# New duration formulas in the planner that orders projections, attention and output projection of a hybrid decoder block

## The chip, the core and the metric

The kernel runs on one core of a Trainium2 chip. The metric is the device time of one execution in microseconds (us). Five engines work from queues of their own, each in the order in which the program issues to it: TensorE (PE, matrix products and transposes), VectorE (DVE), ScalarE (ACT), GpSimd (POOL) and SyncE (SP, which here only issues transfers). An instruction that waits holds up all that stand behind it in its queue.

## What is computed

One block on 1024 tokens of width 1024, float32 (cut to what matters):

```python
h = rmsnorm(x, g_mix_norm)
sb_q, sb_k, sb_v, fx_q, fx_k, fx_v, f_logit, m_q, gate_logit = split(h @ w_in)
o_sb  = stick_breaking_attention(sb_q, sb_k, sb_v)              # 8 heads of 64, causal
o_fox = forgetting_attention(rms(fx_q), rms(fx_k), fx_v, F)     # 8 heads of 64, causal
o_mem = memory_attention(rms(m_q), mk, mv)                      # 4 heads of 128, 256 tokens
gates = sigmoid(gate_logit)                                     # 3 x 1024 columns
merged = gates[0]*(o_sb @ w_sb) + gates[1]*(o_fox @ w_fox) + gates[2]*(o_mem @ w_mem)
x = x + merged @ w_out
u = relu(rmsnorm(x, g_mlp_norm) @ w_ff_up)                      # 1024 -> 4096
x = x + (u*u) @ w_ff_down
```

## The kernel before, in words

Every float32 operand of a product is split into a high part in a shorter format (made by ACT) and a low remainder (made by DVE: operand minus high part), and each product is done three times: high by high, high by low, low by high. So a weight tile `raw`, `ra` or `rb` becomes a pair: `ha`/`la`, `hb`/`lb` or `hc`/`lc`. PE has banks of 128x512 numbers for results: `pp` (three), `sc` (two), `tr` (two), `pv` (one). The large products (the unit products of L1466, the output projection of L2234, the MLP) use a scheme of Strassen's kind: sums and differences of quarters go into seven products, called P1 to P7 in the output projection.

The order of nearly all instructions up to the MLP's first products isn't written out. It comes from a planner in the program (class `Machine`, L186 on), which runs when the kernel is built. Each step of the algorithm is a process that asks for an operation on an engine (`Op`, with an estimated cost), for a buffer (`Get`), or for an event. The planner simulates time: an engine that comes free takes the operation that is ready and due first (due is the time at which it was asked for plus a constant `late` of its process), is busy for its cost, and hands its result on after a fixed tail. An operation of ACT that needs another function table is put off for up to 4.0 us as long as others of the present table are ready (`KEEP`). The order in which the simulation starts operations is the order in which the instructions are issued to the engines; at run time the chip keeps that order, and waits only where data or a buffer isn't ready. Costs change no instruction, only the order (and, since ACT's order changes, the points at which its function table is loaded).

There are two such plans. The first covers the prologue (norm of x, transposes at L475, warm-up transposes at L425), the projections (L1154 for values, gates and branches; L1466 for unit products), the attention (scores and weights at L834 to L944, softmax sums at L622 and L624, memory attention at L657) and two branches. It ends with the fetches of the last branch's operand: heads' outputs `r` are read back (L1673), a second part is fetched (`low_scr`, L1676) and added (L1678), the reciprocal sums are fetched (`l_scr`, L1682) and multiplied in (L1685), and the product is split (L1064 and L1065). The second plan covers the last branch, the output projection, the residual adds (`residual`), the second norm (`normed`: the squares at L2259, the sum at L2278, the root at L373 to L387, the scaling at L2291 on ACT and L2293 on DVE), the turning of the normed rows (`turn_half`, L2316: four transposes of 128x128 into one bank) and the first products of the MLP (L1992). The rest of the MLP, from about 1085 us on, stands in a written order.

All of the costs that the change touches come from three functions of the number of columns, in us: `mm_time` for a product on PE, `act_time` for ACT and `dve_time` for DVE. The cost of transfers (`transfer`, L296: 250 bytes per ns in one pipe, and 2.0 us) stays as it is.

Of the kernel before, what the change touches and what calls it, by code (L numbers as in the profile page):

```python
# [43 lines left out]
def tile_hybrid_block(  # L44
# [240 lines left out]
    spawn = machine.spawn  # L285

    def mm_time(*cols):
        return sum(0.004 + 0.000445 * m for m in cols)

    def act_time(*cols):  # L290
        return sum(0.08 + 0.00083 * m for m in cols)

    def dve_time(*cols):
        return sum(0.08 + 0.00105 * m for m in cols)

    def transfer(fn, size, issue=0.1, rate=250e3, queue_="SP"):  # L296

# [50 lines left out]

    SMALL = 0.19
    PIECE = mm_time(512) * 3  # L350

    def banks(tag):
# [77 lines left out]
    def norm(keys, late, after=None):  # L430
# [21 lines left out]
        for i, key in enumerate(keys):  # L452
            xt, ri, s = x_in[key][0], r[:, i:i + 1], key[1]
            yield spread_
            evs = []
            for k4 in range(2):
                cs = slice(k4 * 512, k4 * 512 + 512) if first else slice(0, D)
                if first or k4 == 0:
                    last = yield Op("DVE", dve_time(512 if first else D), lambda: nc.vector.scalar_tensor_tensor(
                        xt[:, cs], xt[:, cs], ri, gb[:, cs], ALU.mult, ALU.mult), goes_on=True)  # L460
                evs.append(spawn(norm_half(key, xt, k4, last), late))
            for ev in evs:
                yield ev
            XT.put(xt)
            machine.fire((h_made if key[0] == "x" else m_made)[s])

    def norm_half(key, xt, k4, scaled):

        yield scaled
        s, cs = key[1], slice(k4 * 512, k4 * 512 + 512)  # L470
        tr = yield Get(TR)

        def turn():
            for j in range(4):
                nc.tensor.transpose(tr[:, j * P:(j + 1) * P], xt[:, cs][:, j * P:(j + 1) * P], ident)  # L475
        yield Op("PE", 0.44, turn)
        tr4 = tr.rearrange("p (k s) -> p k s", s=P)
        ks4 = slice(4 * k4, 4 * k4 + 4)
        if key[0] == "x":
            hi, lo = (t[:, ks4, s * P:(s + 1) * P] for t in (hTh, hTl))  # L480
        else:
            hi, lo = (t[:, ks4, :] for t in mem_T[s])
        yield Op("ACT", act_time(512), lambda: nc.scalar.activation(hi, tr4, AF.Copy))
        yield Op("DVE", dve_time(512), lambda: nc.vector.tensor_tensor(lo, tr4, f32(hi), ALU.subtract))
        TR.put(tr)
        if key[0] == "x":
            machine.fire(half_made[s, k4])
# [46 lines left out]
    def sums_T():  # L534
        for k in range(4):
            (b11, b12), (b21, b22) = (tuple(tuple(t[:, 4 * k2 + k, c * 512:(c + 1) * 512] for t in (hTh, hTl))
                                            for c in range(2)) for k2 in range(2))
            t1, t2, w_ = yield Get(SN, 3)

            def first():  # L540
                nc.vector.tensor_tensor(t1, f32(b12[0]), f32(b11[0]), ALU.subtract)
                nc.vector.tensor_tensor(w_, f32(b12[1]), f32(b11[1]), ALU.subtract)
                nc.vector.tensor_tensor(t1, t1, w_, ALU.add)

            def second():
                nc.vector.tensor_tensor(t2, f32(b22[0]), t1, ALU.subtract)
                nc.vector.tensor_tensor(t2, t2, f32(b22[1]), ALU.add)

            def third():
                nc.vector.tensor_tensor(w_, t2, f32(b11[0]), ALU.subtract)  # L550
                nc.vector.tensor_tensor(w_, w_, f32(b11[1]), ALU.subtract)
            yield Op("DVE", dve_time(512, 512, 512), first)
            yield Op("DVE", dve_time(512, 512), second)
            two = [spawn(both("P6", k, t2)), spawn(both("P5", k, t1), 2.0)]
            yield Op("DVE", dve_time(512, 512), third)
            two.append(spawn(both("P7", k, w_), 1.0))
            for ev in two:
                yield ev
            SN.put(t1, t2, w_)
# [59 lines left out]
    def sums_kept(h0):  # L619

        cols = fn[:, 8 * h0:8 * h0 + 16]
        yield Op("DVE", SMALL, lambda: nc.vector.reciprocal(cols, cols))  # L622
        tr = yield Get(TR)
        yield Op("PE", 0.12, lambda: nc.tensor.transpose(tr[:16, :P], cols, ident))  # L624
        t = yield Get(OB)
        yield Op("ACT", act_time(P), lambda: nc.scalar.activation(t[:16, :P], tr[:16, :P], AF.Copy))
        TR.put(tr)
        yield Op("SP", 0.1, lambda: nc.sync.dma_start(
            l_scr[h0:h0 + 2, :].rearrange("h (i p) -> (h i) p", p=P), t[:16, :P]), 2.5)
        OB.put(t)  # L630

    def mem_attention(h, half, kv, q):
# [8 lines left out]
        def scores_of(t2):  # L641
            sc = yield Get(SC)
            mx = st[:, 4 + 2 * t2:6 + 2 * t2]

            def scores():
                for j in range(2):
                    ts_ = slice((2 * t2 + j) * P, (2 * t2 + j + 1) * P)
                    mm3(sc[:, j * MEM:(j + 1) * MEM],
                        [((qh[:, ts_], ql[:, ts_]), (kh[:, h2, :], kl[:, h2, :]))])

            def maxima():
                nc.vector.tensor_reduce(mx, sc.rearrange("p (t m) -> p t m", m=MEM), AX.X, ALU.max, negate=True)

            def exps():
                for j in range(2):
                    t = 2 * t2 + j
                    nc.scalar.activation(pr[:, t, :], sc[:, j * MEM:(j + 1) * MEM], AF.Exp,  # L657
                                         bias=mx[:, j:j + 1], accum_out=l[:, t:t + 1])
            yield Op("PE", 6 * mm_time(256), scores)
            yield Op("DVE", dve_time(512), maxima)  # L660
            yield Op("ACT", act_time(256, 256) + 0.34, exps, table=AF.Exp)
            SC.put(sc)
# [15 lines left out]
        def block(j):  # L678
            if j == 0:
                pv[0] = yield Get(PV)  # L680
            else:
                yield turned[0]
            tr = yield Get(TR)

            def turn():
                for t in range(4):
                    nc.tensor.transpose(tr[:, t * P:(t + 1) * P], pr[:, t, j * P:(j + 1) * P], ident)
            yield Op("PE", 0.44, turn)
            machine.fire(turned[j])
            ph = yield Get(PH)  # L690
            yield Op("ACT", act_time(512), lambda: nc.scalar.activation(ph, tr, AF.Copy))
            pl = yield Get(PL)
            yield Op("DVE", dve_time(512), lambda: nc.vector.tensor_tensor(pl, tr, f32(ph), ALU.subtract))
            TR.put(tr)
            yield products_[j]
            cs = slice(h2 * P, (h2 + 1) * P)
            ab = passes((vh[:, j, cs], vl[:, j, cs]), (ph, pl))
            result = yield Op("PE", 3 * mm_time(512), products(pv[0], ab, j == 0, j == 1), goes_on=True)
            machine.fire(products_[j + 1])
            yield result  # L700
            PH.put(ph)
            PL.put(pl)
# [2032 lines left out]
```

## Time and profile before

| | |
|---|---|
| time, median of 3 runs | 1667.45 us (1667.15 to 1668.06) |
| profiled execution, its own time | 1668.89 us |
| span of that execution in the profile | 1667.1 us |
| PE busy, products and transposes | 1654.5 us, 9118 instructions |
| DVE busy | 1292.5 us, 2079 instructions |
| ACT busy | 848.9 us, 1474 instructions |
| POOL busy | 256.3 us, 440 instructions |
| transfers | 284.32 MB, mean 171 GB/s |

The profile gives, for each engine, when each instruction ran and what ended the idle time before it. Durations of products overlap: a product of 512 columns is listed with 389 ns, though the next may begin sooner. A stretch of the time can be asked for by itself; its row gives the busy time and count of each engine, the clock granted to PE as a share of full speed, the share in which transfers ran, and the bytes that they moved.

### The profile page before, as it was taken

To read this page: it belongs to the slowest core of one execution; us is meant where nothing else is said; L and a number is where in the kernel's file an instruction comes from. 1 tells how busy PE (TensorE), PEld (TensorE's weight loads), DVE (VectorE), ACT (ScalarE), POOL (GpSimd) and SP (SyncE) were. 2 spreads that over 40 slices of the span, in tenths; PEclk is the share of its full clock that TensorE was granted. 3 is DMA by queue.
4 is the path that set the end of the run, shared out by engine and by line. 5 is a ranking of instruction groups with operands and counts; after the bars stand their busy time and mean duration, and the time that the engine had idled before them with its cause. 6 is when DMAs were issued, how large, how long until landed. Compare 5 with 4: busy or idle time off the path is not lost.

```text
span 1667.1 us, 24994 instructions
## 1 busy us (share of the span) xinstructions
PE 1654.5 (99%) x9118; PEld 1434.6 (86%) x9118; DVE 1292.5 (78%) x2079; ACT 848.9 (51%) x1474; POOL 256.3 (15%) x440
## 2 busy tenths in 40 slices
PE   9999999999999999999999999999999999999999
PEld 9998899998888888888888887878888888888887
DVE  7978778855459889868878798987777776787875
ACT  6445555535458898877761446533333345333331
POOL 0001000000153142245400011011122120000000
PEclk9999999999999999999999999999999999999999
DMA  7445534468474455577747643144444475564532
GB/s 247 149 161 170 165 114 137 141 182 255 140 237 145 147 160 162 140 222 222 244 142 215 219 168 104 58 158 150 148 158 158 151 275 211 181 213 169 202 126 76
DMA packets 142222, 284.32 MB, mean 171 GB/s; under 512 B 16914, under 2 KB 53330, under 8 KB 142099
## 3 DMA queue, kind: packets, MB, share of 16 engines
q1 hardware_dynamic: 110562, 183.08, 32.5%
q0 software_dynamic: 31536, 99.64, 19.9%
q8 instruction: 72, 1.18, 0.3%
q14 instruction: 52, 0.42, 0.1%
HBM read 189.83 MB, written 92.83 MB: 170 GB/s over the span
## 4 chain that ended last, share of the span: by engine, by line
PE 72%; issue 14%; DVE 7%; POOL 3%; DMA 3%; ACT 1%; SPq 0%; POOLq 0%; ACTq 0%; DVEq 0%
PE pp L1466 11%; PE pp L1154 10%; PE sc L1466 7%; PE pp L2672 7%; PE sc L1154 6%; PE tr L927 4%; PE tr L2672 4%; PE sc L2672 4%; POOL s_scr L2009 3%; PE pv L1466 3%; PE pv L2672 2%; PE sc L944 2%; PE pp L944 2%; DVE h L1928 2%; DVE tmp L1928 1%
## 5 line engine op out<-in xcount | busy, mean ns | idle before, releaser
L1992 PE MATMUL pp<-h,oh 128*128 128x512 f32 x384 | 118.7, 390 | 1.2 <-ACT cu L2077 0.9
L934 DVE TENSOR_TENSOR ptl<-tr,pth 128x512 fp32r<-128x512 f32 (+1 forms) x160 | 99.0, 628 | 23.9 <-ACT pth L932 23.1
L932 ACT ACTIVATE pth<-tr 128x512 fp32r<-128x512 f32 (+1 forms) x160 | 87.4, 557 | 33.5 <-PE sc L944 14.6
L1992 PEld LDWEIGHTS pp<-h,oh 128*128 128x128 f32 x384 | 71.9, 188 | 17.2 <-ACT cu L2077 1.7
L1383 POOL DMA_DIRECT2D raw<-w_in x32 | 24.2, 757 | 394.8 <-DVE la L1065 207.6
L1992 PE MATMUL pp<-h,ol 128*128 128x512 f32 x192 | 74.9, 390 | 0.0
L853 DVE TENSOR_TENSOR_SCAN e<-r,e 128x384 f32<-128x384 f32 (+3 forms) x64 | 66.3, 1044 | 6.8 <-ACT e L838 6.4
L2672 PE MATMUL pp<-h,h 128*128 128x512 f32 x288 | 66.6, 389 | 0.0
L2672 PE MATMUL pp<-sop,sop 128*128 128x512 f32 x288 | 66.6, 389 | 0.0
L2672 PEld LDWEIGHTS pp<-sop,sop 128*128 128x128 f32 x288 | 54.1, 188 | 11.2
L2672 PEld LDWEIGHTS pp<-h,h 128*128 128x128 f32 x288 | 54.1, 188 | 11.2
L927 PE MATMUL tr<-ident,e 128*128 128x128 f32 x416 | 62.5, 272 | 0.0
L927 PEld LDWEIGHTS tr<-ident,e 128*128 128x128 f32 x416 | 50.5, 140 | 9.9 <-DVE ptl L934 0.2
L2009 POOL DMA_DIRECT2D s_scr<-cu x48 | 26.1, 544 | 191.7 <-DVE cu L1999 183.6
L1014 POOL DMA_DIRECT2D h<-sbk_scr x64 | 33.3, 526 | 95.5 <-PE pv L151 29.5
L944 PE MATMUL sc<-pth,v 128*128 128x256 f32 (+1 forms) x170 | 47.4, 301 | 0.0
L2587 ACT ACTIVATE h<-t 128x2048 fp32r<-128x2048 f32 (+1 forms) x9 | 15.4, 1725 | 60.2 <-DVE t L1928 56.1
L1154 PE MATMUL sc<-h,hc 128*128 128x512 f32 (+1 forms) x154 | 44.8, 375 | 0.0
L1928 DVE TENSOR_TENSOR x<-x,pp 128x512 f32<-128x512 f32 x39 | 26.6, 682 | 22.8 <-PE pp L2672 22.8
L1065 DVE TENSOR_TENSOR lb<-raw,hb 128x1024 fp32r<-128x1024 f32 x20 | 24.5, 1223 | 25.6 <-ACT hb L1064 25.5
L2009 POOL DMA_DIRECT2D s_scr<-s x60 | 32.5, 542 | 71.4 <-DVE s L1928 64.8
L1992 PEld LDWEIGHTS pp<-h,ol 128*128 128x128 f32 x192 | 36.0, 188 | 8.1 <-DVE ol L1928 0.6
(792 smaller groups left out, 5540.3 us busy)
## 6 DMA issues: line engine op xcount, KB each, us to landing
ur<-s_scr SPq DMA_DIRECT2D x26, 1024.0 KB
raw<-w_in POOLq DMA_DIRECT2D x32, 512.0 KB, 4.8
raw<-w_up SPq DMA_DIRECT2D x60, 256.0 KB
s_scr<-s POOLq DMA_DIRECT2D x60, 256.0 KB, 2.7
g<-w_down SPq DMA_DIRECT2D x14, 1024.0 KB
s_scr<-cu POOLq DMA_DIRECT2D x48, 256.0 KB, 2.9
h<-sbk_scr POOLq DMA_DIRECT2D x64, 128.0 KB, 3.1
o<-gate_scr SPq DMA_DIRECT2D x32, 256.0 KB
```

Source lines behind the costliest of these rows:

```text
L853: nc.vector.tensor_tensor_scan(out=back, data0=rho[:, :u][:, ::-1], data1=back, initial=0.0 if last else beta[:, c + u:c + u + 1], op0=ALU ...
L927: nc.tensor.transpose(tr[:, jj * 256 + a * P:jj * 256 + (a + 1) * P], es[a][:, j * P:(j + 1) * P], ident)
L932: yield Op("ACT", act_time(512 - lo_c), lambda: nc.scalar.activation(ph[:, lo_c:], tr[:, lo_c:], AF.Copy))
L934: yield Op("DVE", dve_time(512 - lo_c), lambda: nc.vector.tensor_tensor(pl[:, lo_c:], tr[:, lo_c:], f32(ph[:, lo_c:]), ALU.subtract))
L944: nc.tensor.matmul(pv[0][:, c_:256], pair.v[:, j, b, :], p_[:, jj * 256 + c_:(jj + 1) * 256], start=(k == 0 and n_ == 0 and i == 0), stop= ...
L1014: nc.gpsimd.dma_start(f32(t[k][rows_, :]), src)
L1154: nc.tensor.matmul(ps, a_, b_, start=(first and i == 0), stop=(last and i == n - 1))
L1466: nc.tensor.matmul(out_, a_, b_, start=(first and n == 0 and j == 0), stop=(last and n == 3 and j == len(todo) - 1), skip_group_check=True)
L1928: nc.vector.tensor_tensor(out_, a_, b_, op)
L1992: nc.tensor.matmul(ps, w[a_][:, k * P:(k + 1) * P], h[b_][k], start=(first and k == 0 and i == 0), stop=(last and k == 3 and i == 2), skip ...
L2009: nc.gpsimd.dma_start(s_scr[r0:r0 + P, :], t)
L2672: nc.tensor.matmul(ps, a_[:, c, qs], b_[:, c, :], start=(kind in ("P1", "P2", "P7") and c == 0 and i == 0), stop=(kind in ("P2", "P4", "P3 ...
```

## The change

The constants of the three formulas are replaced. Nothing else is edited.

```diff
     def mm_time(*cols):
-        return sum(0.004 + 0.000445 * m for m in cols)
+        return sum(0.0133 + 0.0004167 * m for m in cols)
 
     def act_time(*cols):
-        return sum(0.08 + 0.00083 * m for m in cols)
+        return sum(0.09 + 0.00093 * m for m in cols)
 
     def dve_time(*cols):
-        return sum(0.08 + 0.00105 * m for m in cols)
+        return sum(0.07 + 0.00113 * m for m in cols)
```

By these, a product of 512 columns is planned with 0.227 us where it was 0.232, one of 256 with 0.120 (0.118); an operation of 512 columns on ACT with 0.566 (0.505) and on DVE with 0.649 (0.618); one of 1024 columns with 1.042 (0.930) and 1.227 (1.155). So PE is planned a little quicker on wide products, and ACT and DVE slower. The instructions stay the same ones on PE, DVE, POOL and SP. ACT has two more table loads, 26 instead of 24: one more at L657 (exponentials of the memory attention) and one more at L837 (the first step of the stick-breaking weights). The order moves on all engines, in many places by a few rows. Three places follow.

**PE, where the second norm's first rows are turned.** `L2316` are the transposes; `L2234` with `sc_9651` and `sc_9652` are products of the output projection that follow the `pv_9655` ones. Before:

```order
L2234 MATMUL pv_9655<-ha_9904,ol_9896 128x512
L2234 MATMUL sc_9651<-hb_10013,cu_9931 128x512
L2234 MATMUL sc_9651<-lb_10015,cu_9931 128x512
L2234 MATMUL sc_9651<-hb_10013,cu_9935 128x512
L2316 MATMUL pp_9648<-ident,h_9632 128x128 x4
L2316 MATMUL pp_9649<-ident,h_9632 128x128 x4
L2234 MATMUL sc_9651<-hb_10013,cu_9932 128x512
L2234 MATMUL sc_9651<-lb_10015,cu_9932 128x512
L2234 MATMUL sc_9651<-hb_10013,cu_9936 128x512
L2316 MATMUL pp_9650<-ident,h_9632 128x128 x4
```

And now, from the seventh product after `pv_9655` on:

```order
L2234 MATMUL sc_9651<-ra_9998,cu_9963 128x512
L2234 MATMUL sc_9651<-rb_10000,cu_9963 128x512
L2234 MATMUL sc_9651<-ra_9998,cu_9967 128x512
L2234 MATMUL sc_9651<-ra_9998,cu_9964 128x512
L2234 MATMUL sc_9651<-rb_10000,cu_9964 128x512
L2234 MATMUL sc_9651<-ra_9998,cu_9968 128x512
L2234 MATMUL sc_9652<-hb_9997,cu_9961 128x512
L2234 MATMUL sc_9652<-lb_9999,cu_9961 128x512
L2234 MATMUL sc_9652<-hb_9997,cu_9965 128x512
L2316 MATMUL pp_9648<-ident,h_9632 128x128 x4
L2316 MATMUL pp_9649<-ident,h_9632 128x128 x4
L2234 MATMUL sc_9652<-hb_9997,cu_9962 128x512
```

Between the last `pv_9655` product and the first turn there stood three products; now there stand fifteen (the six not shown are the first six of `sc_9651`).

**DVE, on the way to the first turn's operand.** `h_9632` and `h_9633` are rows of the residual, `L2278` to `L387` the sum and root of the norm, `L2293` the scaling; `h_9959` and `h_9936` are sums of quarters of an MLP weight, `ol` low parts for P4. Before:

```order
L1928 TENSOR_TENSOR h_9632<-h_9632,pp_9649 128x512
L1928 TENSOR_TENSOR h_9959<-h_9958 128x512
L1928 TENSOR_TENSOR h_9959<-h_9958,h_9959 128x512
L2278 TENSOR_REDUCE st_10079<-fn 128x2
L1928 TENSOR_TENSOR h_9633<-h_9633,pp_9650 128x512
L378 TENSOR_SCALAR st_10091<-st_10079 128x2
L381 RECIPROCAL st_10084<-st_10084 128x2
L385 TENSOR_TENSOR st_10092<-st_10084 128x2
L386 TENSOR_TENSOR st_10092<-st_10092,st_10091 128x2
L387 SCALAR_TENSOR_TENSOR st_10093<-st_10092,st_10084 128x2
L2293 SCALAR_TENSOR_TENSOR h_9632<-h_9632,st_10093,gb_9636 128x512 x2
```

And now:

```order
L1928 TENSOR_TENSOR ol_10028<-g_7040,oh_10024 128x512
L1928 TENSOR_TENSOR h_9633<-h_9633,pp_9650 128x512
L1928 TENSOR_TENSOR ol_10029<-g_7041,oh_10025 128x512
L378 TENSOR_SCALAR st_10081<-st_10073 128x2
L1928 TENSOR_TENSOR ol_10030<-g_7041,oh_10026 128x512
L381 RECIPROCAL st_10076<-st_10076 128x2
L385 TENSOR_TENSOR st_10082<-st_10076 128x2
L386 TENSOR_TENSOR st_10082<-st_10082,st_10081 128x2
L387 SCALAR_TENSOR_TENSOR st_10083<-st_10082,st_10076 128x2
L1928 TENSOR_TENSOR h_9633<-h_9633,pv_9655 128x512
L1928 TENSOR_TENSOR h_9936<-h_9935,h_9936 128x512
L2293 SCALAR_TENSOR_TENSOR h_9632<-h_9632,st_10083,gb_9636 128x512
```

The four low parts for P4, which stood ahead of this place, now stand in the chain; the sums and products that stood ahead of the residual add moved out of it, and two operations of 512 columns come between L387 and L2293.

**ACT, at the first weights of the second pair's values.** `hc_169<-rb_166` is the high part of these weights, for which PE's products at L1154 wait; `L1064 h_...<-sn` are high parts of another operand, `L1647` empties a gate's bank. Before:

```order
L1064 ACTIVATE h_757<-sn_150 128x512
L1064 ACTIVATE h_755<-sn_149 128x512
L1647 ACTIVATE sn_142<-sc_137 128x512
L1064 ACTIVATE hc_169<-rb_166 128x1056
L1064 ACTIVATE h_759<-sn_141 128x512
```

And now:

```order
L1647 ACTIVATE sn_142<-sc_137 128x512
L1064 ACTIVATE hc_169<-rb_166 128x1056
L1064 ACTIVATE h_747<-sn_150 128x512
L1064 ACTIVATE h_745<-sn_149 128x512
L1064 ACTIVATE ha_163<-ra_164 128x1056
```

The two high parts from `sn`, which stood ahead of the bank's emptying and of the weights, now stand behind both.

## Prediction

> **What bounds the kernel now.** I read the page first.
>
> ```profile
> span 1667.1 us, 24994 instructions
> PE 1654.5 (99%) x9118; PEld 1434.6 (86%) x9118; DVE 1292.5 (78%) x2079; ACT 848.9 (51%) x1474; POOL 256.3 (15%) x440
> ```
>
> PE works 1654.5 of 1667.1 us. The change leaves PE's instructions as they are, so the work doesn't shrink; a new order can only win what PE loses to waits (12.6 us) and to a lower clock, or add to it. So I asked where PE is idle: a table by stretches of the program, where the column after the window is PE's busy time.
>
> ```profile
> 0.00:25.00 25.00, 23.00 (x168) 21.96 (x169) 17.10 (x44) 16.42 (x31) 0.70 (x6) 1.00 0.96 333
> 55.00:60.00 5.00, 4.30 (x33) 3.89 (x32) 4.98 (x8) 2.96 (x5) 0.00 (x0) 1.00 0.95 288
> 475.00:880.00 405.00, 404.21 (x2528) 356.38 (x2527) 331.59 (x710) 317.26 (x710) 137.95 (x250) 1.00 0.61 181
> 880.00:1012.00 132.00, 131.44 (x580) 108.48 (x579) 115.14 (x162) 50.32 (x72) 10.56 (x7) 1.00 0.57 192
> 1012.00:1028.00 16.00, 13.05 (x60) 10.71 (x58) 14.86 (x31) 10.35 (x22) 0.00 (x0) 0.89 0.47 148
> 1085.00:1110.00 25.00, 23.77 (x101) 18.39 (x100) 21.75 (x33) 8.58 (x16) 4.88 (x9) 1.00 0.44 147
> ```
>
> Idle by difference: 2.00 at the start, 0.70 at 55 to 60, 0.79 in the whole attention (475 to 880), 0.56 in branches and first half of the output projection, 2.95 at 1012 to 1028, 1.23 at 1085 to 1110. Most of the rest lies after 1110, in the written order, which the change doesn't touch. The waits of PE say for whom:
>
> ```profile
> PE pp L2316 <- ACT h L2291: 3.0, 1, 3.0
> PE pp L1992 <- ACT cu L2077: 0.9, 2, 0.7
> PE pv L879 <- DVE st L884: 0.7, 1, 0.7
> PE pp L1154 <- DVE lc L1065: 0.6, 1, 0.6
> PE sc L2234 <- DVE rb L1928: 0.6, 1, 0.6
> ```
>
> One wait is worth more than the others together: the first turn of normed rows. Its stretch in steps, with the clock as the number after POOL's:
>
> ```profile
> 1017.00:1020.10 3.10, 0.55 (x3) 0.13 (x1) 2.96 (x11) 2.11 (x6) 0.00 (x0) 1.00 0.70 202
> 1020.10:1021.30 1.20, 0.79 (x6) 0.80 (x7) 1.20 (x3) 1.20 (x2) 0.00 (x0) 0.84 1.10 203
> 1021.30:1022.50 1.20, 1.20 (x6) 1.10 (x6) 1.20 (x2) 1.20 (x4) 0.00 (x0) 0.50 0.90 328
> 1022.50:1023.70 1.20, 1.20 (x6) 0.90 (x5) 0.95 (x3) 1.20 (x3) 0.00 (x0) 0.50 1.04 401
> 1023.70:1025.00 1.30, 1.30 (x7) 1.17 (x6) 1.05 (x2) 1.30 (x4) 0.00 (x0) 0.76 0.23 82
> ```
>
> After the wait PE counts as busy, but at a granted clock of 0.50 to 0.84. Lost to that: 1.20 x 0.16 + 1.20 x 0.50 + 1.20 x 0.50 + 1.30 x 0.24 = 1.70 us. So **this place costs 2.95 + 1.70 = 4.65 us**.
>
> **The turn, step by step.** The timeline there (start, duration, engine, line):
>
> ```profile
> 1017.16 0.39 PE L2234 MATMUL sc<-hb,cu 128*128 128x512 f32 x1
> 1018.94 0.60 ACT L2259 ACTIVATE pp<-h 128x512 f32<-128x512 f32 x1 [0.30 <-DVE h L1928]
> 1019.47 0.16 DVE L387 SCALAR_TENSOR_TENSOR st<-st,st 128x2 f32<-128x2 f32 x1
> 1019.67 1.41 DVE L2293 SCALAR_TENSOR_TENSOR h<-h,st,gb 128x512 f32<-128x512 f32 x2
> 1019.73 0.72 ACT L2291 ACTIVATE h<-h,st 128x512 f32<-128x512 f32 x1
> 1020.36 1.04 ACT L2136 ACTIVATE hc<-h 128x1024 fp32r<-128x1024 f32 x1
> 1020.51 1.20 PE L2316 MATMUL pp<-ident,h 128*128 128x128 f32 x6 [2.95 <-ACT h L2291]
> ```
>
> PE has issued its third product by 1017.39 and then stands until 1020.51, for ACT's scaling, which follows DVE's L387 (end 1019.63). The new order puts twelve more products ahead of the turn. What one of 512 columns costs PE comes from a stretch in which all are such:
>
> ```profile
> 1120.00:1142.70 22.70, 22.70 (x102) 18.81 (x101) 18.07 (x28) 7.03 (x13) 4.34 (x8) 1.00 0.48 162
> ```
>
> 22.70 / 100 (102 are counted with those cut at both ends) is 0.227 us, so PE now comes to the turn at 1017.39 + 12 x 0.227 = 1020.11. The operands: on DVE the same work stands ahead of L387 as before but for one sum of 512 columns, about 0.68 less by the rows of such operations (L2293: 1.41 for two), so L387 ends near 1019.0 to 1019.1. On ACT the high part L2136 (1.04) now stands ahead of the first L2291. L2259 follows its residual add, which ends some 1.2 earlier, near 1017.7, since one low part and the root's steps now lie behind that add; L2259 (0.60 and its read of 0.19) ends near 1018.5, L2136 near 1019.5, the first L2291 (0.72) at 1020.0 to 1020.3. The first turn waits 0 to 0.2. The second needs DVE's L2293, behind two operations of 512 columns: 1019.05 + 3 x 0.65 = 1021.0, against PE at 1020.6: 0.4 more. Together 0.4 to 0.7, and I take 0.65. Two shorter waits don't look like one of 2.95; the wait of 0.6 for rb (row above) is the nearest in size, and there the granted clock stayed up:
>
> ```profile
> 973.50:978.00 4.50, 3.94 (x18) 2.93 (x17) 4.50 (x7) 0.88 (x2) 0.00 (x0) 1.00 0.05 19
> ```
>
> So the turn goes from 4.65 to 0.65: **-4.0**. Until the end of the output projection everything on PE is then 4.0 earlier, and what is late next is DVE. It has room for that in the 57 us after the turn (51.19 of 57), with the end of the projection inside them:
>
> ```profile
> 1028.00:1085.00 57.00, 57.00 (x278) 47.33 (x276) 51.19 (x90) 33.40 (x61) 7.43 (x8) 1.00 0.17 61
> ```
>
> 5.8 us idle against 4.0: enough, and then the waits of 1085 to 1110 stay as they are. If that cover were gone, up to 4.0 would come back there.
>
> The Trainium skill ("TensorE: Matmul & The Clock Gate", Part 1: The HAM clock gate) says the array falls to half clock after an idle window of about 3.4 us and needs about 3.4 us of work to rise, in windows that run freely. The trace agrees in part: 2.95 us of idling sufficed, and the 0.50 lasted about 3 us. By that page short waits would cost nothing but themselves, as the row at 973 has it; the sum is the same.
>
> **The first weights of the second pair's values.**
>
> ```profile
> 53.31 1.15 ACT L1064 ACTIVATE h<-sn 128x512 fp32r<-128x512 f32 x2 [4.24 <-DVE sn L547]
> 54.85 1.07 ACT L1064 ACTIVATE hc<-rb 128x1056 fp32r<-128x1056 f32 x1
> 55.95 1.26 DVE L1065 TENSOR_TENSOR lc<-rb,hc 128x1056 fp32r<-128x1056 f32 x1
> 57.27 0.39 PE L1154 MATMUL pp<-lc,h 128*128 128x264 f32 x1 [0.64 <-DVE lc L1065]
> ```
>
> ACT idles 4.24 us for `sn`, does two high parts, empties a bank, then makes `hc`; `lc` ends at 57.21, and PE waits. In the new order bank and `hc` stand ahead of the two high parts. ACT can then start them inside the 4.24, so `lc` no longer ends last: **-0.7** by the idle of 55 to 60, and up to -1.1 with the small delays of the products behind it. I take -0.9. What is late next is those high parts, by ACT's 0.58 and 1.07; their users stand well behind on PE.
>
> **Start (0 to 25).** DVE's and PE's first steps change places: the first product's low part comes later, the transposes earlier. Followed row by row the first rows of products end within 0.2 of where they did. I take 0, between -0.4 and +0.4.
>
> **Attention.** Here the order moves most: counted in PE work from the start (each product of the order at its own duration, 0.227 for 512 columns), the last score product goes from 693 to 709 and the last product with values (L944) from 863 to 876, so that ACT and DVE have some 13 to 16 us more for the same work. That can win no more than the 0.79 that PE idles there. Against it stand the two more table loads on ACT:
>
> ```profile
> L657 ACT ACT_TABLE_LOAD x8 | 10.3, 1283 | 0.1
> L837 ACT ACT_TABLE_LOAD x7 | 9.0, 1283 | 0.1
> ```
>
> 2 x 1.28 = 2.57 us of ACT. ACT works 317 of the 405 us of that stretch, so 88 us of gaps hide them; without that cover they would cost 2.57. The range is -0.8 (all waits gone) to +2.6, and nearest is 0, since PE lost only one wait in 2528 products in an order that knew less of the durations.
>
> The Trainium skill ("ScalarE: Activation LUTs", What ACT_TABLE_LOAD costs) counts a drain of 1.38 us beside the 1.28, so 5.3 us for two, which speaks against this change. The trace has only the 1.28, with 0.1 idle ahead of it. By the page the upper end would be +5.3 and the value still 0, inside the same 88 us.
>
> **From attention to the last branch.** The work that PE can do without the last pair's operand shrinks: behind L624, 111 products (25.2 us) stand ahead of the last branch's first use where 171 (38.8 us) stood. The last pair's way, as now seen:
>
> ```profile
> 894.63 1.09 SPq L1682 DMA_DIRECT2D e<-l_scr  x2
> ...
> 901.73 1.23 DVE L1685 TENSOR_TENSOR r<-r,e 128x1024 f32<-128x1024 f32 x1 [0.63 <-DMA e<-l_scr]
> ```
>
> 7.1 us from issue to use, and now 15 us to spare. In the new order, from L624 on: on DVE the sum L1678 runs behind an eviction and `lb` at +14.2 to +15.3; SP issues the two fetches of `l_scr` at +15.5 behind three gate fetches; landing +22.6; L1685 to +23.8; splits at +26.7 and +27.9 behind two more evictions. PE uses them at +27.5 and +30.2. **0.85 us to spare**, so 0, and each us beyond that costs one. A slow fetch is seen in the chain:
>
> ```profile
> 729.43 8.29 DMA r<-o_scr
> ```
>
> At 8.29 instead of 7.1 PE would wait 0.3. I take +0.2, between 0 and +1.5.
>
> **Sum.** -4.0 - 0.9 + 0 + 0 + 0.2 = -4.7 on the profiled execution's 1668.89 us: 1664.2. That execution was 1.44 above the median of 1667.45, so the median comes to **1662.8 us**. The measurement can tell about 0.2%, 3.3 us, from no change.
>
> **Rivals**, in medians. (a) *The turn's gain is given back on DVE.* DVE is busy 14.86 of 16 us at the turn; if the projection's end comes 4.0 earlier but the splits behind it don't, the waits at 1085 to 1110 grow by up to 4.0: 1666.8, the same. For: only 5.8 us are free there. Against: these lie ahead of the written part. 0.14. (b) *The turn waits longer and the clock falls all the same.* If ACT's L2136 or the two operations ahead of L2293 run later than I count, by 1 us, and the clock's 1.70 is lost again: 1662.8 + 2.7 = 1665.5, the same. For: ACT has 1.04 more in the chain. Against: the row at 973. 0.12. (c) *The last pair's operand decides.* It is on a chain of two fetches, three DVE steps and two evictions. If `l_scr` takes twice its 7.1 us, since three gate fetches and the output projection's weights now go with it, and L1685 misses its place behind one pair of evictions (1.4), PE waits 8.5 - 0.85 = 7.65, and the clock falls for 1.70: 1662.8 - 0.2 + 9.35 = 1672.0, **slower**; it decides from some 7 us of lateness on. For: cover of 15 us is gone. Against: of the fetch now only 0.63 is waited for, and only by DVE. 0.10. (d) *Nothing but scattered waits changes places*: both gains are real in the order, but new waits of the size of the 0.6 to 0.9 rows turn up in 9118 rearranged products, five of them: 1662.8 + 3.5 = 1666.3, the same. 0.06.
>
> **How the numbers follow.** My forecast has 0.58, with 1660.9 to 1664.5 as its own range (the ends of the terms: start 0.4, attention 0.8, weights 0.2, turn 0.5 downward; the junction's 1.3 and 0.4 upward). The range must leave out no more than 2 in 10: 1660.5 to 1668.5 takes in (a), (b) and (d). Faster means under 1664.1: 0.60. Within 0.2%: 0.29. Slower than 1670.8: 0.11, (c) and a little for what I don't see.
>
> **What would show it.** Turn right: PE's wait for L2291 under 0.4, one for L2293 under 0.6, clock 1.00 throughout. Weights right: no wait of L1154 for `lc`. Junction right: no wait of L1154 in the 30 us behind the last L624. (a) shows as waits of L1992 above 1.3 us in all; (c) as a wait of L1154 for L1065 with `r` before the last branch. What would make it wrong most simply is a wait of several us at a place where PE lost nothing before.

## The result, and the profile after

The changed kernel takes **1683.57 us** (median of 5 runs, 1682.91 to 1684.17), the kernel before 1667.54 us in the same series: a ratio of 1.0093, with a 95% interval of 1.0078 to 1.0108. It is 16 us slower; 4.7 us faster was forecast, and the range ended at 1668.5. The two executions that were profiled lie 14.1 us apart (1682.98 and 1668.89 us). The page of the profile of the changed kernel:

```profile
span 1681.2 us, 24988 instructions
PE 1657.2 (99%) x9118; PEld 1432.0 (85%) x9118; DVE 1297.0 (77%) x2079; ACT 853.7 (51%) x1476; POOL 254.8 (15%) x440
```

PE's work is the same to 0.2%, and the span is 14.1 us longer: PE waits more. The same stretches as before the change, in the same columns (PE's busy time stands after the window). The first turn of normed rows now starts at 1035.7 us, 15.2 later than before, so its stretch is 1027 to 1043 here, where it was 1012 to 1028:

```profile
0.00:25.00 25.00, 21.43 (x171) 20.93 (x172) 15.88 (x38) 15.60 (x29) 0.70 (x6) 1.00 0.94 336
25.00:55.00 30.00, 28.28 (x235) 27.47 (x235) 23.36 (x50) 16.74 (x34) 0.00 (x0) 1.00 0.47 139
55.00:60.00 5.00, 5.00 (x44) 5.00 (x43) 4.96 (x7) 3.33 (x6) 0.00 (x0) 1.00 0.73 234
475.00:880.00 405.00, 396.28 (x2439) 346.26 (x2439) 322.35 (x688) 310.16 (x686) 138.26 (x251) 1.00 0.59 178
1027.00:1043.00 16.00, 15.61 (x75) 12.52 (x74) 15.79 (x31) 10.02 (x22) 1.30 (x1) 1.00 0.45 149
```

The two places on which the forecast was built behave as it said: at 55 to 60 PE is never idle (0.70 before), and at the turn it is idle for 0.39 us (2.95) at a clock of 1.00 (0.89). But the attention, 475 to 880, which had 0.79 us of idle PE, has 8.72, and 25 to 55, which had none, has 1.72. (0 to 25 has 3.57 for 2.00, but loses no more than before when it is counted from start to start, as in the table below: 4.3 against 4.5.) PE's waits name the places:

```profile
PE tr L927 <- DVE ptl L934: 6.2, 7, 1.7
PE tr L475 <- DVE xt L459: 1.7, 1, 1.7
PE pp L149 <- ACT es L838: 1.4, 1, 1.4
PE pp L944 <- DVE ptl L934: 1.2, 2, 0.7
PE tr L475 <- DVE g L484: 1.1, 1, 1.1
PE pp L2316 <- ACT tmp L2323: 0.6, 1, 0.6
PE pp L2316 <- DVE h L2293: 0.4, 1, 0.4
```

The first, third and fourth row are the attention's own steps (transposing the weights, multiplying them with the values). None of these was in the list before. Stretch by stretch, first of the kernel before, then of the changed one:

```profile
710.00:730.00 20.00, 20.00 (x130) 17.68 (x128) 12.02 (x33) 15.49 (x35) 10.93 (x21) 1.00 0.69 192
730.00:750.00 20.00, 19.31 (x112) 16.20 (x111) 15.45 (x42) 14.38 (x33) 9.15 (x17) 1.00 0.87 268
```

```profile
710.00:730.00 20.00, 14.85 (x91) 11.75 (x90) 17.11 (x38) 17.62 (x39) 14.22 (x27) 1.00 0.68 203
730.00:750.00 20.00, 16.44 (x111) 13.47 (x110) 15.02 (x41) 16.66 (x37) 10.53 (x20) 1.00 0.83 229
```

8.7 of the 40 us are idle. What is missing there shows when one asks for the products of L1154 alone. In this part of the program most of those are projections of gates and branches: they depend on nothing of the attention that is still running, and the planner gives them to PE only when no other step is ready for it (they are marked `side`). I call them spare products. (The same line also has the memory attention's own products with its weights `pth` and `ptl`, which aren't spare.) Before, then after (PE's busy time with that line alone):

```profile
690.00:710.00 20.00, 11.76 (x45) 7.73 (x43) 1.00 0.65 183
710.00:730.00 20.00, 11.54 (x43) 7.45 (x43) 1.00 0.69 192
730.00:750.00 20.00, 10.05 (x37) 6.16 (x35) 1.00 0.87 268
```

```profile
690.00:710.00 20.00, 12.21 (x48) 8.72 (x48) 1.00 0.22 71
710.00:730.00 20.00, 2.15 (x8) 0.99 (x6) 1.00 0.68 203
730.00:750.00 20.00, 2.84 (x10) 1.62 (x11) 1.00 0.83 229
```

From 710 to 750 PE had 80 products of this line and now has 18, and 12 of the 18 are the memory attention's own (6 of the 80). Of the spare ones, the last for a gate (`g`) and the first for the memory branch (`ha`) stand so in the changed kernel (durations in ns, then the first and the last start):

```profile
L1154 PE MATMUL pv<-g,lb x4: 389/393/395, 706.7 to 710.0; 128*128 128x512 f32 x4
L1154 PE MATMUL sc<-ha,hc x1: 395/395/395, 743.8 to 743.8; 128*128 128x512 f32 x1
```

From 710.0 to 743.8 no spare product starts, some 34 us; before, the two were at 738.1 and 738.3. The spare products aren't gone; they have run already. Counted in the order, 182 us of products of L1154 stood ahead of the 780th attention product, and 202 us stand there now. The next ones belong to the memory branch, which opens only when the memory attention's outputs are back. In between PE has nothing but the attention, and goes at the pace of its chain through ACT and DVE. A piece of that chain of waits:

```profile
711.00 1.28 ACT L837
712.58 0.37 ACT e L838
712.95 0.49 ACT r L837
713.44 0.49 ACT e L838
713.93 0.49 ACT pth L691
```

The first line is a table load; then sigmoids and copies stand on the path one after another, with PE idle.

For all runs below, what PE loses is counted from the start of one product to the start of the next, against 0.227 us for 512 columns, 0.177 for 384, 0.123 for 264, 0.120 for 256 and 0.109 for a transpose; so it holds idle time and slow products alike. In us, by stretch of each run's own profile (between 60 and 475, and from 1135 on, the sums are under 1 in these kernels except for the first of them in `issue_intervals`, 2.0; the stretches don't move with the program, so in runs that come there some 14 us late a wait can fall into the next column):

| run | 0–60 | 475–690 | 690–790 | 790–950 | 950–1010 | 1010–1060 | 1060–1135 | all |
|---|---|---|---|---|---|---|---|---|
| before | 5.7 | 1.1 | 1.9 | 0.8 | 0.8 | 5.1 | 2.4 | 17.3 |
| after | 6.8 | 1.0 | 13.7 | 2.7 | 0.9 | 2.7 | 4.2 | 31.4 |
| `plan1_old` | 5.5 | 1.1 | 2.4 | 0.8 | 1.7 | 2.0 | 4.0 | 17.0 |
| `plan2_old` | 7.0 | 1.0 | 13.6 | 2.2 | 0.8 | 4.9 | 2.6 | 31.2 |
| `loads_4_more` | 5.6 | 3.3 | 3.9 | 0.4 | 1.0 | 3.8 | 2.5 | 19.9 |
| `spare_rationed` | 6.6 | 6.7 | 3.4 | 0.6 | 1.9 | 1.3 | 4.1 | 25.3 |
| `spare_early` | 5.9 | 1.6 | 16.9 | 0.4 | 0.8 | 3.6 | 2.6 | 31.2 |
| `issue_intervals` | 5.6 | 2.8 | 0.6 | 0.4 | 1.7 | 5.2 | 2.3 | 20.3 |
| `act_alone` | 6.1 | 0.6 | 23.8 | 1.8 | 0.3 | 4.0 | 2.6 | 39.8 |
| `mm_alone` | 5.7 | 1.0 | 16.1 | 0.5 | 0.6 | 2.2 | 2.6 | 28.6 |
| `dve_alone` | 5.1 | 1.8 | 14.9 | 0.9 | 0.7 | 3.5 | 2.5 | 28.9 |
| `turn_later` | 5.5 | 1.1 | 1.8 | 0.4 | 0.8 | 5.0 | 2.4 | 16.6 |
| `second_mm` | 5.6 | 1.1 | 1.5 | 0.4 | 0.7 | 2.8 | 2.5 | 15.0 |
| `second_dve` | 5.5 | 1.1 | 0.9 | 0.4 | 1.3 | 5.7 | 2.2 | 16.9 |

After less before is 14.1, the growth of the span. 11.8 of it lies at 690 to 790, where both of the table loads that the change adds lie too (five there, three before), 1.9 at 790 to 950, 1.1 in the first 60; at 950 to 1135, where 4.0 were to be won, the balance is -0.5.

### The profile page after: what moved, and what is told of

Read it like the earlier page. It is cut to its first block, busy times and chain, and to the rows that moved or that the text cites. A ratio compares the mean times of both kernels' runs of the same rounds, so it can differ in the third digit from the quotient of the medians.

```text
span 1681.2 us, 24988 instructions
## 1 busy us (share of the span) xinstructions
PE 1657.2 (99%) x9118; PEld 1432.0 (85%) x9118; DVE 1297.0 (77%) x2079; ACT 853.7 (51%) x1476; POOL 254.8 (15%) x440
## 4 chain that ended last, share of the span: by engine, by line
PE 83%; DVE 8%; issue 3%; DMA 2%; ACT 2%; POOL 1%; SPq 0%; POOLq 0%; DVEq 0%; ACTq 0%
PE pp L1466 11%; PE pp L1992 8%; PE pp L2672 7%; PE sc L1466 7%; PE sc L1154 6%; PE pv L1154 5%; PE pp L1154 5%; PE sc L1992 4%; PE pp L944 4%; PE tr L2672 4%; PE sc L2672 4%; PE tr L927 3%; PE pv L1466 3%; PE pv L2672 2%; DVE h L1928 2%
## 5 line engine op out<-in xcount | busy, mean ns | idle before, releaser
L1992 PE MATMUL pp<-h,oh 128*128 128x512 f32 x384 | 118.7, 390 | 1.2 <-ACT cu L2077 0.9
L944 PE MATMUL pp<-pth,v 128*128 128x256 f32 x320 | 88.2, 298 | 0.0
L1992 PEld LDWEIGHTS pp<-h,oh 128*128 128x128 f32 x384 | 71.8, 188 | 17.6 <-ACT cu L2077 1.7
L944 PE MATMUL pp<-ptl,v 128*128 128x256 f32 x320 | 79.4, 282 | 1.3 <-DVE ptl L934 1.2
L1992 PE MATMUL pp<-h,ol 128*128 128x512 f32 x192 | 74.9, 390 | 0.3 <-DVE ol L1928 0.3
L944 PEld LDWEIGHTS pp<-ptl,v 128*128 128x128 f32 x320 | 60.9, 190 | 3.9 <-DVE ptl L934 2.3
L944 PEld LDWEIGHTS pp<-pth,v 128*128 128x128 f32 x320 | 60.4, 189 | 2.2
L1154 PE MATMUL sc<-h,hc 128*128 128x512 f32 (+1 forms) x160 | 46.7, 376 | 0.0
```

What stands on the lines that cost most here:

```text
L944: nc.tensor.matmul(pv[0][:, c_:256], pair.v[:, j, b, :], p_[:, jj * 256 + c_:(jj + 1) * 256], start=(k == 0 and n_ == 0 and i == 0), stop= ...
L1154: nc.tensor.matmul(ps, a_, b_, start=(first and i == 0), stop=(last and i == n - 1))
L1992: nc.tensor.matmul(ps, w[a_][:, k * P:(k + 1) * P], h[b_][k], start=(first and k == 0 and i == 0), stop=(last and k == 3 and i == 2), skip ...
```

## The experiments

Theory A: the higher prices of ACT and DVE make the planner believe that attention steps aren't ready, so it gives PE spare products sooner, and they run out before the memory branch opens. Rival B: the two table loads more. (The profile counts 26 loads before and 28 after; the section on the change has 24 and 26, two too few each.) Rival C: the second plan. Rival D: ACT and DVE are as slow as the new formulas say and set the pace whatever the order. Lines inserted into a kernel shift its line numbers by a few.

**Each plan by itself.** The formulas are switched between the plans:

```diff
+    COST = (old formulas, new formulas)   # plan2_old: the other way round
+    plan = [0]
     def mm_time(*cols):
-        return sum(0.004 + 0.000445 * m for m in cols)
+        a, b = COST[plan[0]][0]
+        return sum(a + b * m for m in cols)
...
+    plan[0] = 1
+    PIECE = mm_time(512) * 3
```

> First plan with the old formulas, second plan with the new ones. Theory A (the loss of 700 to 750 was laid down by the first plan, because its higher ACT and DVE costs spend the spare products too early): the profile up to the first output projection product is that of before (738 us: one wait of 0.7), the time is before plus what the second plan does alone, -4.0 at the turn and +3.3 behind it: 1667 +- 1. Rival B (two more table loads on ACT): the loads are 26 again, so the same 1667. Rival C (the second plan is at fault, its changed transfers reach back): 1675 or more.

> First plan with the new formulas, second plan with the old ones. Theory A and rival B: the waits of 700 to 750 stay, the turn waits 3 us as before and the waits behind it shrink, 1683.6 + 4.0 - 3.3 = 1684.3 +- 1. Rival C: 1668.

Measured: `plan1_old` 1668.20 us against 1668.23 for before, ratio 1.000 (0.999 to 1.001); `plan2_old` 1683.81, ratio 1.0101 (1.0086 to 1.0116). The whole loss comes from the first plan, and C falls. The second plan's change is worth nothing that these runs can tell: in the table it saves 3.1 at 1010 to 1060 and loses 0.9 ahead of it and 1.6 behind.

**More table loads.** Ahead of two late sigmoid steps in the kernel before:

```diff
             def sigmoids():
+                if 684 < machine.now < 685 or 699.5 < machine.now < 700:
+                    nc.scalar.activation(extra_[:, :1], one, AF.Exp)
```

> The kernel before, with four table loads more: ahead of two late sigmoid steps of the stick-breaking attention one exponential of a single column is put, so that the table is loaded there and back. The order of all else is that of before. Theory A: 4 x 1.28 = 5.1 us of ACT are covered, 1667.5 to 1669. Rival B: two loads were worth some 11 us, so four cost 10 us or more: 1677 or above.

Measured: 1672.01 us, ratio 1.003 (1.0017 to 1.0043): between the two. Both places show among the waits of PE:

```profile
PE pv L834 <- ACT e L841: 2.0, 1, 2.0
PE pv L150 <- ACT es L841: 1.3, 1, 1.3
```

So a pair of loads that falls into this part costs some 2 us, more than theory A allowed (it took ACT's gaps for cover, but those lie elsewhere). For the two loads that the change adds, that makes some 2 of the 11.8 us, an estimate: they lie at another place, where there is no spare work beside them.

**The spare products spread out, with all new formulas.** In the planner's loop over engines:

```diff
+                    if (engine == "PE" and ready and ready[0][3].side and 500 < self.now < 770
+                            and self.side > 463 + 0.385 * (self.now - 500)):
+                        continue
                     if ready and not self.busy[engine]:
```

> All new formulas, and a ration in the first plan: from 500 to 770 us of its own clock the spare products may not run ahead of 463 + 0.385 us per us. Theory A: the costs only matter through the order, so with the spare products spread out PE's waits at 700 to 750 (11.6 us more than before) and at 882 (2.2) go, and since ACT and DVE are really quicker than the plan says few waits come in their place: 1683.6 - 13.8 + 1 = 1671, between 1669 and 1674. Rival B: loads are as many or one less, 1680 or above. Rival D (ACT and DVE really are as slow as the new formulas say, and set the end of attention whatever the order): the waits only move ahead, 1682 or above.

Measured: 1677.00 us, ratio 1.0057 (1.0042 to 1.0072). The loss at 690 to 790 falls from 13.7 to 3.4 and that at 790 to 950 from 2.7 to 0.6, as theory A says, though the loads are 28, as after the change, and again five of them lie at 690 to 790. But 5.7 come back at 475 to 690, where the ration now makes PE wait; half of the gain that I expected. Rationing by a straight line is a poor order too.

**The spare products spent early, with all old formulas.** The opposite:

```diff
+            if engine == "PE" and 500 < self.now < 720 and self.side < 466 + 0.46 * (self.now - 500):
+                spare = [item for item in self.ready[engine] if item[3].side]
+                if spare:
+                    self.ready[engine].remove(min(spare))
+                    self.ready[engine].append((False, -1e9, 0, min(spare)[3], min(spare)[4]))
+                    heapify(self.ready[engine])
             _, _, _, op, proc = self.choose(self.ready[engine])
```

> All old formulas, but in the first plan PE takes a spare product first, from 500 to 720 us of the plan's clock, as long as fewer than 466 + 0.46 us per us have run: that is the rate at which the new formulas spend them. Theory A: the spare products end at about 710, and PE waits at 700 to 760 as after the change, 10 to 14 us; 1676 to 1682, although no cost was changed. If the costs act in another way than by spending spare products (rival B by loads, rival D by slower engines): near before, 1670 or less.

Measured: 1683.13 us, ratio 1.0093 (1.0078 to 1.0108), the same as the change, with no cost changed. PE's time with L1154 (here L1160), as above:

```profile
690.00:710.00 20.00, 11.93 (x45) 7.71 (x43) 1.00 0.18 57
710.00:730.00 20.00, 1.72 (x6) 1.06 (x6) 0.94 0.67 192
730.00:750.00 20.00, 2.00 (x7) 1.26 (x8) 0.98 0.66 199
```

The same hole, and 16.9 us lost at 690 to 790. This shows theory A at work: when the spare products run is enough to make the loss. It has 28 loads, as after the change, which leaves the loads' share of some 2 us open.

**Other prices.** ACT and DVE by the interval at which their instructions follow one another in the trace of before, and each formula of the change alone:

```diff
-        return sum(0.09 + 0.00093 * m for m in cols)
+        return sum(0.05 + 0.00083 * m for m in cols)
...
-        return sum(0.07 + 0.00113 * m for m in cols)
+        return sum(0.065 + 0.00104 * m for m in cols)
```

> Both plans with ACT and DVE priced by the interval at which such instructions follow one another in the trace of before (ACT 0.05 + 0.00083 m, so 0.475 at 512; DVE 0.065 + 0.00104 m, 0.597 at 512), PE as in the change. It has 28 table loads, as after the change. Theory A: spare products last as in before, no wait over 2 us at 700 to 760, 1664 to 1669. Rival B (28 loads are what costs): 1677 or above.

> Only ACT's new formula (30 table loads). Theory A: spare products are spent as fast as after the change (556 against 557 us of them at 700), so waits of 8 to 13 us at 720 to 790: 1676 to 1682. If DVE's price is what did it: 1670 or less.

> Only PE's new formula (26 loads). Theory A: spare products go as in before up to 720 (554 against 554), and run short only at 750 to 770: 4 to 8 us there, 1670 to 1676. If only ACT's and DVE's prices matter: 1666 to 1669.

> Only DVE's new formula (28 table loads). Theory A: in the plan the spare products are gone for 17 us (735 to 752; 36 us after the change, 42 in the run that spent them early, 9 + 12 with PE's formula alone, which cost 15): some 10 us of waits at 735 to 775, 1675 to 1681. If DVE's price is harmless: 1668.

Measured: `issue_intervals` 1671.68, ratio 1.0021 (1.0012 to 1.0031); `act_alone` 1689.14, 1.0126 (1.0111 to 1.0141); `mm_alone` 1681.69, 1.0084 (1.0064 to 1.0103); `dve_alone` 1682.07, 1.0082 (1.0068 to 1.0096). With issue intervals the loss at 690 to 790 is 0.6, with 28 loads, so B can't be the main cause; its 3 us of extra loss lie elsewhere (2.2 in the projections, 1.7 more in the attention's first part, 0.9 at 950 to 1010), and the time missed the expected 1664 to 1669. Each of the three formulas alone costs 14 to 21 us, more than I expected of any. `mm_alone` has 26 loads and prices ACT and DVE as before, so neither loads nor those prices are needed. Its hole is short and deep, and the clock falls in it:

```profile
750.00:775.00 25.00, 20.35 (x71) 15.36 (x70) 13.66 (x37) 12.11 (x26) 7.87 (x16) 0.66 0.87 267
```

By the prediction's way of counting, 20.35 us of busy PE at a clock of 0.66 lose 20.35 x 0.34 = 6.9 us, an estimate, beside the 4.65 us idle. A good part of this loss is therefore the clock's, which stayed at 1.00 after the change.

So the statement "higher prices of ACT and DVE spend the spare products" was too narrow: a shift of prices can move the point at which they run out, or the one at which the next ones open. In `mm_alone` the gates' products last to 743.0, longer than before (738.1); but the memory attention's last products come at 738.5 (715.3 before), and the first of the memory branch at 750.3. The longest stretch at 680 to 800 between the starts of two spare products puts the runs in two groups. It is 5.1 us before, 5.1 in `loads_4_more`, 4.2 in `spare_rationed` and 4.7 in `issue_intervals`, and at 690 to 790 these lose 0.6 to 3.9 us. It is 33.9 after the change, 40.6 in `spare_early`, 44.0 in `act_alone`, 19.3 in `dve_alone` and 12.9 in `mm_alone`, and these lose 13.7 to 23.8. The loads don't part them: `issue_intervals` has five at 690 to 790, `mm_alone` and `dve_alone` three, as before. But within the second group the length of that stretch alone doesn't tell what it costs (12.9 us cost more in `mm_alone` than 33.9 after the change).

**The turn by itself, and the second plan with other prices.** In the kernel before, the first turns get a later due time; then first plan old, second plan with one formula changed:

```diff
-            for ev in [spawn(turn_half(s, k4), -2.0 + 0.5 * k4) for k4 in range(2)]:
+            for ev in [spawn(turn_half(s, k4), (3.0 if s < 2 else -2.0) + 0.5 * k4) for k4 in range(2)]:
```

> The kernel before (all old formulas), with the turns of the first two row blocks given a later due time (3.0 for -2.0), so that the first turn comes twelve products later, where the change has it. If the turn's gain is real and only the rest of the new second plan gave it back: no wait over 1 us at the turn, clock 1.00 through, and 4 us less in all, 1664 (ratio 0.9975). If the gain is taken back by whatever waits behind the turn, whichever plan: 1667 to 1668, with the waits of PE at 1025 to 1125 grown by 3 to 4.

> First plan with the old formulas, second with PE's new formula alone; the first turn comes nine products later than before. In the run with PE's formula alone PE lost 5.4 us from 950 to 1125 against 8.3 in before: 1668.0 - 2.9 = 1665 (ratio 0.998), if the second plan's gain doesn't hang on where the first ended; 1668 if it does.

> First plan with the old formulas, second with DVE priced by its issue interval (0.065 + 0.00104 m) and the rest old; the first turn comes fifteen or more products later than before. If cover ahead of the turn is what counts: 1664 to 1666. If the gain is taken back behind it as with all three new formulas: 1667 to 1669.

Measured: `turn_later` 1668.25, ratio 1.000 (0.9991 to 1.0008); `second_mm` 1666.11, 0.9987 (0.9979 to 0.9996); `second_dve` 1669.44, 1.0011 (1.0002 to 1.002). In `turn_later` the wait for the first turn shrinks, and another takes its place, at a later turn:

```profile
PE pp L2316 <- ACT tmp L2323: 2.5, 1, 2.5
```

The stretches of that run, 1012 to 1020 and on:

```profile
1012.00:1020.00 8.00, 7.75 (x35) 6.08 (x35) 7.86 (x17) 3.31 (x9) 0.00 (x0) 1.00 0.41 125
1020.00:1028.00 8.00, 5.60 (x30) 4.41 (x30) 7.84 (x16) 8.00 (x16) 1.72 (x1) 1.00 0.47 172
1028.00:1050.00 22.00, 21.95 (x108) 18.34 (x109) 16.27 (x34) 13.96 (x32) 3.88 (x3) 0.92 0.23 85
```

At 1020 to 1028 DVE is busy for 7.84 and ACT for 8.00 of 8 us. By this, these two set the pace there, and the twelve products put ahead of the first turn only moved the wait. The other two differ from what their expectations say of them: against the three products ahead of the first turn in the kernel before, `second_mm` has nine and `second_dve` none. Their waits for that turn follow: 1.8 and 3.7 (3.0 before), and the losses at 1010 to 1060 are 2.8 and 5.7 (5.1). So the one order with six products (1.36 us) more ahead of the turn keeps its gain, and the two with twelve more (`turn_later`, `plan1_old`) don't. That the six are the reason isn't shown, since the rest of the second plan differs too. `second_mm` beats the kernel before, by 0.13% (0.04 to 0.21%).

## Why the prediction was wrong, point by point

*What bounds the kernel*: right. PE's work didn't change, and the time is what PE loses.

*The turn, -4.0*: right at its place, wrong in what it is worth. The first turn has no wait in the list, the second waits 0.4 for L2293, and the clock stayed at 1.00, as forecast; a wait of 0.6 (for L2323) stands at a later turn. But "5.8 us idle against 4.0: enough" doesn't follow from a mean over 57 us: DVE's idle time lay at 1028 to 1050 (16.38 of 22 busy before), while the wait that came in `turn_later` lies in 8 us where ACT and DVE are full, and in `plan1_old` the losses lie ahead of 1010 and behind 1060. `plan1_old` gives the term as 0.0, within some 1.7 us. That is rival (a) in its effect, but not by its sign: the listed waits of L1992 make 1.4 us (1.3 before), and what came behind 1060 is spread over delays of under 0.9.

*The weights of the second pair, -0.9*: right; PE's idle time at 55 to 60 went from 0.70 to 0.

*The start, 0*: wrong. I followed the first rows to their products and stopped; at 34 to 42 PE waits for DVE's transposed rows (L484, 1.1 of it in one wait). With the weights' gain the first 60 us cost 1.1 more. No run takes this apart; `act_alone` shows a like loss (1.6 between 25 and 50) and `mm_alone` and `dve_alone` don't.

*The attention, 0 between -0.8 and +2.6*: **this step failed**. It had seen that the attention's last products come 13 to 16 us of PE work later, and read it as time won for ACT and DVE. Where there is a fixed stock of other work, it says instead that this much of the stock has been used ahead of its time. The bound of +2.6 priced only the added loads, and took PE's one wait in 2528 products as a sign of slack; but the traces show that order to be one in which the stock lasted just long enough (738.1 to 738.3). The loss was 11.8 at 690 to 790, some 2 of it, by the estimate above, from the loads. The prediction's last sentence names a wait of several us at a place where PE lost nothing before; it came as many waits of 1.4 us at most.

*From attention to the last branch, +0.2*: the slack was counted at the wrong step. No wait on the fetch of `l_scr` shows; the last attention products themselves wait 1.7 for DVE's `ptl` at 882.

*The rival (c), slower*: the sign came true, its mechanism didn't; there was no term for PE running out of work that depends on nothing.

The Trainium skill's rule on table loads ("ScalarE: Activation LUTs", What ACT_TABLE_LOAD costs), 2.66 us a switch, spoke against the change, but isn't what decided. In `loads_4_more` a pair takes 2.8 us on ACT, from 678.72 to 681.51, with the one-column exponential in between:

```profile
678.10 0.60 ACT L692 ACTIVATE pth<-tr 128x512 fp32r<-128x512 f32 x1
678.72 1.28 ACT L839 ACT_TABLE_LOAD   x1
680.01 0.20 ACT L839 ACTIVATE st<-sm 128x1 f32<-128x1 f32 x1
680.22 1.28 ACT L840 ACT_TABLE_LOAD   x1
681.51 0.28 ACT L840 ACTIVATE r<-pv 128x128 f32<-128x128 f32 x1
```

So a switch costs 1.3 here, and the page's drain isn't seen beside it.

What stays open: how the 11.8 us divide between the bare chain and the one more pair of loads in it (some 2 by `loads_4_more`), and why the clock fell in `mm_alone` and not after the change.

## What to carry to other kernels

Where a planner fills gaps greedily from a stock of independent work, a change of its prices must be judged by when that stock runs out: count, at each milestone of the critical chain, how much of it has been spent in both orders, and when the next opens, before counting any wait that goes. Better measured prices needn't give a better order: prices nearer to the trace's durations lost 0.93%, issue intervals 0.21%, and one formula alone up to 1.26%. And a wait removed is a gain only if the engine it waited for isn't full over the next stretch, which is to be asked of stretches of a few us, not of a mean over 57.

## What was not expected of the hardware

The clock didn't fall in the changed kernel though PE was idle for 5.15 of 20 us at 710 to 730 (1.00 throughout, with waits of 1.4 us at most), nor in `spare_rationed` at a wait of 1.9 us (1.00 at 745 to 750 and 750 to 775). But it had a mean of 0.66 in `mm_alone` at 750 to 775 (20.35 of 25 busy), where the longest wait is 1.8 us, and 0.94 in `spare_early` at 710 to 730, where the longest is 1.3; and it fell to 0.50 in the kernel before after 2.95 us. The length of a single wait alone doesn't tell when. So the prediction's reading of the row at 973, that short waits cost nothing but themselves, doesn't hold for several of them close together.
